# Matmul order inside a weight unit, and eight placements of the moving tiles

## The chip, the cores and the metric

The kernel runs on one core of a Trainium2 chip. The metric is the device time of one execution in microseconds (us). Times before are the median of three runs; the profile is of one more execution.

## The reference

One inference step of a decoder trunk of one layer, width 2048, for 256 prompt tokens and 8 x 4 sample tokens (288 token columns in all). Three sub-layers follow each other, each inside RMS norms: a SwiGLU feed-forward pair, a hybrid mixer (a gated linear attention group and an HGRN2 group, both recurrences), and a second SwiGLU pair.

```python
x = x + 0.5 * rmsnorm(swiglu(rmsnorm(x, g[0]), ffn1_w_in, ffn1_w_out), g[1])
m, sg, sh = hybrid_mixer(rmsnorm(x, g[2]), mix_w_in, ..., mix_w_out, s_gla, s_hgrn)
x = x + rmsnorm(m, g[3])
x = x + 0.5 * rmsnorm(swiglu(rmsnorm(x, g[4]), ffn2_w_in, ffn2_w_out), g[5])
# swiglu(x) = (silu(x @ w_gate) * (x @ w_up)) @ w_out, hidden width 5632
```

Everything is float32, and the weights are large: 364 MB are read from memory.

## The kernel before, in words

Activations lie transposed: a tile holds 128 features (partitions) by 288 tokens, so x is 16 tiles (`KT = 16`). To reach float32 accuracy with the faster float32r matmul, each operand is split into a high and a low part, and a product is three matmuls, recorded at L596, L597 and L598: weights high by x high, weights high by x low, weights low by x high. The parts of x are `xh[k]` and `xl[k]`; those of the hidden layer are `hh` and `hl`.

The class `Weights` streams the weights in units of 128 x 1024 numbers: SyncE loads a unit (`raw`, 3 buffers), ACT writes its high part (L100) and DVE its low part (L101) into a `wh` buffer (`hl` in the code, 4 buffers, at times 2 more on the other side of the memory). One buffer holds two halves `a` of `HALF = 1024 + 32` numbers, each with 512 high numbers, 512 low numbers and a gap of 32. A unit covers two tiles of x (`k` and `k + 1`, one half each) for four output tiles of 128 features.

The function `block` computes four output tiles (`f = 0..3`) over `nk` tiles of x: `nk / 2` units, the products of one output tile being summed in one bank. It walks the units in order. In all but the last unit it takes `k` outermost and `f` inside; in the last unit (`tail`) it takes `f` outermost and `k` inside, and evacuates each output tile (`evac`) as it is finished. After each `k` it calls `tick(k)`, in which other blocks' work is issued: squares for a norm, steps of the recurrence, splits. The feed-forward stages are made of `gate`, `up` (8 units each, on x) and `out` blocks (2 units each, on the hidden tiles); the mixer has blocks `qk`, `v`, `hfq`, `hi`, `gate` and `mo`, all on x or on the mixer's output, which takes the place of x in `xh` and `xl`. The first block of each stage (`gate1_0`, `qk0`, `gate2_0`) has orders of its own: `fill` puts products that are ready early first, `late` holds some back.

The order on each engine is the order of issue, with marks (`issue_after`) that place an instruction behind another; there is no loop at run time. In the mixer's last gate block `tick_last` writes the high and low parts of the mixer's output `y` over `xh` and `xl` (`split_y`), tile by tile, as soon as the block has read them.

In the program, each partition holds first `x`, `y`, then `xh[0..15]`, `xl[0..15]`, `rt`, `rp`, `acc`, `cols`, then the raw buffers and the weight buffers. A tile of x takes 288 x 4 = 1152 bytes. The extra weight buffers and the fill tiles lie at the other end, behind a tile named `gap`, and their places follow its size.

Of the kernel before, what the change touches and what calls it, by code (L numbers as in the profile page):

```python
# [9 lines left out]
F32 = mybir.dt.float32  # L10
F32R = mybir.dt.float32r
# [5 lines left out]
P = 128  # L17
TP = 256
TS = 32
T = TP + TS  # L20
# [3 lines left out]
KT = D // P  # L24
# [106 lines left out]
def trunk_kernel(ctx, tc, x_prompt, x_sample, state_gla, state_hgrn, norm_gains, f1_in, f1_out, f2_in, f2_out,  # L131
# [6 lines left out]
    xpool = ctx.enter_context(tc.tile_pool(name="xpool", bufs=1))  # L138
# [104 lines left out]
    FIRST = 2  # L243
# [4 lines left out]
    x = [xpool.tile([P, T], F32, name=f"x{k}") for k in range(KT)]  # L248
    yg = [xpool.tile([P, 4, T], F32, name=f"y{k}") for k in range(4)]
    y = [yg[k // 4][:, k % 4, :] for k in range(KT)]  # L250
    xh = [xpool.tile([P, T], F32R, name=f"xh{k}") for k in range(KT)]
    xl = [xpool.tile([P, T], F32R, name=f"xl{k}") for k in range(KT)]
    rt = xpool.tile([P, T], F32, name="rt")
    rp = xpool.tile([P, T], F32, name="rp")
    acc = xpool.tile([P, T], F32, name="acc")
    cols = xpool.tile([P, 16], F32, name="cols")

    def gain(i, k):
        return prm[:, i * KT + k:i * KT + k + 1]
# [324 lines left out]

    product = [None]

    def block(name, nk, rhs, evac, width=512, tick=None, tail=1, hold=False, most=99, fill=None, late=0):

        nf, per = width // P, 1024 // width
        nu = nk // per  # L590
        ps = [mmtile(f"{name}_{f}") for f in range(nf)]
        ws = [W.next() for _ in range(EARLY // per)] if fill else []

        def mm3(dst, w, f, k, parts, start, stop):
            a, c = k % per, slice(f * P, f * P + P)
            yield lambda: PE.matmul(dst, w[0][:, a, c], parts[0], start=start, stop=False)  # L596
            yield lambda: PE.matmul(dst, w[0][:, a, c], parts[1], start=False, stop=False)  # L597
            yield lambda: PE.matmul(dst, w[1][:, a, c], parts[0], start=False, stop=stop)  # L598

        def mm(w, f, k):  # L600
            if not fill or f or k >= EARLY:
                for ready in mm3(ps[f][:, 0:T], w, f, k, rhs(k), k == 0, k == nk - 1):
                    product[0] = ready().ins

        if fill:
            fill.products(lambda dst, k, parts, stop: mm3(dst, ws[k // per], 0, k, parts, k == 0, stop), ps[0][:, 0:T])
        for u in range(nu - tail):
            w = ws.pop(0) if ws else W.next()
            for k in range(u * per, (u + 1) * per):
                if fill and k < UPDATED:  # L610

                    fs = range(1 if k < EARLY else 0, nf)
                    threes = [list(mm3(ps[f][:, 0:T], w, f, k, rhs(k), k == 0, False)) for f in fs]
                    for three in threes:
                        three[0]()
                        product[0] = three[2]().ins
                    with tc.issue_after(product[0]):
                        for three in threes:
                            product[0] = three[1]().ins
                elif k < late:  # L620

                    threes = [list(mm3(ps[f][:, 0:T], w, f, k, rhs(k), k == 0, False)) for f in range(nf)]
                    for ready in [r for t in threes for r in t[:2]] + [t[2] for t in threes]:
                        product[0] = ready().ins
                else:
                    for f in range(nf):
                        mm(w, f, k)
                if tick is not None:
                    tick(k)
            W.ahead(most)  # L630
            if fill and u == 5:
                fill.scaled()
        ws = [W.next() for _ in range(tail)]
        ks = range((nu - tail) * per, nk)
        ticked = 0
        for f in range(nf):
            for k in ks:
                mm(ws[k // per - (nu - tail)], f, k)
            evac(f, fill.total(ps[f][:, 0:T]) if fill and f == 0 else ps[f][:, 0:T])
            while tick is not None and (ticked + 1) * nf <= (f + 1) * len(ks):  # L640
                tick(ks[ticked])
                ticked += 1
        if not hold:
            W.ahead()
# [4 lines left out]
    def ffn(tag, gcol, gnext, pn, before, fill=None):  # L649
# [3 lines left out]
        with ExitStack() as pools:  # L653
# [3 lines left out]
            def do_in(c):  # L657
                hh = fp.tile([P, 4, T], F32R, name=f"hh{tag}_{c}", tag="hh")
                hl = fp.tile([P, 4, T], F32R, name=f"hl{tag}_{c}", tag="hl")
                hid[c] = (hh, hl)  # L660
                gs = []

                def gate(g):
                    def run():
                        V.tensor_tensor(g, g, rt, op=ALU.mult)
                        act(g, g, AF.Silu)
                    return run

                def ev_gate(f, ps):
                    g = fp.tile([P, T], F32, name="g", tag="g", bufs=6)  # L670
                    gs.append(g)
                    if c == 0:
                        W.behind = S.activation(g, ps, AF.Copy).ins
                        pn.late.append(gate(g))
                    else:
                        V.tensor_tensor(g, ps, rt, op=ALU.mult)
                        act(g, g, AF.Silu)

                def ev_up(f, ps):
                    u = fp.tile([P, T], F32, name="u", tag="u", bufs=3)  # L680
                    V.tensor_tensor(u, ps, rt, op=ALU.mult)  # L681
                    V.tensor_tensor(u, u, gs[f], op=ALU.mult)
                    S.activation(hh[:, f, :], u, AF.Copy)
                    V.tensor_tensor(hl[:, f, :], u, hh[:, f, :].bitcast(F32), op=ALU.subtract)

                if c == 0:
                    block(f"gate{tag}_0", KT, xrhs, ev_gate, tick=pn.tick0, most=1 if final else 0, fill=fill,
                          late=0 if final else FIRST)
                    before.close()
                    if not final:  # L690
                        border.append(Border(mixer_start, hg1, gnext, 5, 2))
                else:
                    block(f"gate{tag}_{c}", KT, xrhs, ev_gate)
                if final and c == 0:
                    last_pool()
                block(f"up{tag}_{c}", KT, xrhs, ev_up, tick=pn.tick1 if c == 0 else None)
# [170 lines left out]
    def mixer(pn, border):  # L867
        with ExitStack() as mx:
# [667 lines left out]
            for g in range(2):  # L1536
                d = group_tiles(f"g{g}")
                block(f"qk{g}", KT, xrhs, ev_gla(d, g == 0), tick=tick if g else pn.tick0, most=99 if g else 1,
                      fill=None if g else border.fill)
                if g == 0:  # L1540
                    scan_pool()
                if g == 0:
                    vt = vtiles("g0")
                    block("v0", KT, xrhs, ev_v(*vt, 2, yg[1]), 
                          tick=lambda k: (pn.tick1(k), scale_lr() if k == 8 else a_lr() if k == 10 else lr_parts() if k == 12 else None))
                    with tc.issue_after(W.recent[0]), tc.issue_after(W.recent[1]):
                        lower_bounds()

                    turns.insert(0, lambda d=d: gla_decay(d, 0))
                else:  # L1550
                    turns.extend([lambda d=d, f=f: gla_decay(d, 1, (f,)) for f in range(2)])
                    vt = vtiles("g1")
                    block("v1", KT, xrhs, ev_v(*vt, 2, yg[1]), tick=tick)
                gens.append((g, scan(d, *vt, True, 4 * g, state_gla[0][:, 2 * g:2 * g + 2],
                                     sgp[0, 0, 2 * g:2 * g + 2], sgs[0][:, 2 * g:2 * g + 2]), True))
# [42 lines left out]
            def split_y(t):  # L1598
                S.activation(xh[t], y[t], AF.Copy)
                V.tensor_tensor(xl[t], y[t], xh[t].bitcast(F32), op=ALU.subtract)  # L1600
# [6 lines left out]
                    tick(k)  # L1607

            def tick_last(k):
                if k < 12:  # L1610
                    split_y(k)

            for n in range(4):
                block(f"gate{n}", KT, xrhs, ev_gate(n), tick=(tick, tick, tick_silu, tick_last)[n])
# [22 lines left out]
    class Border:  # L1637


        def __init__(self, n, gains, gnext, some, ahead=0):  # L1640
            self.pools = ExitStack()
            top = self.pools.enter_context(tc.tile_pool(name=f"top{gnext}", bufs=1, side="right"))
            top.tile([P, 56], F32, name=f"gap{gnext}")
            W.begin_extra(self.pools.enter_context(tc.tile_pool(name=f"hx{gnext}", bufs=2, side="right")), wider(n))
            self.fill = Fill(self.pools.enter_context(tc.tile_pool(name=f"fl{gnext}", bufs=1, side="right")),
                             f"fill{gnext}", gains, gnext, some, ahead)
# [47 lines left out]
```

## Time and profile before

| what | us |
|---|---|
| median of 3 runs | 2227.61 |
| lowest and highest run | 2226.94, 2229.22 |
| the profiled execution | 2226.28 |
| its span | 2224.5 |
| TensorE matmul busy | 2212.8 (17,820 matmuls) |
| TensorE weight load busy | 2197.9 (17,820) |
| VectorE (DVE) busy | 1386.7 |
| ScalarE (ACT) busy | 1020.1 |
| GpSimd (POOL) busy | 180.2 |

The span is the time from the first to the last instruction of the profiled execution; the execution's own time has 1.8 us around it. Busy times are those of instructions in flight. Matmuls are pipelined, so one matmul's duration (about 290 ns) covers parts of its neighbours; how fast they follow each other is read from the differences of their starts. A row of the timeline has the start, the duration, the engine, the line, the operation and its operands; a row of the groups has the count behind the x, then busy us and the mean ns of one, then the idle time before. A row of the waits says who waited for whom, for how many us in all, how often, and the longest.

### The profile page before, as it was taken

Reading aid. Unit: us, or ns where it says so; the run is one execution under the profiler, and the core shown is the slowest. Engines: PE = TensorE matmul, PEld = TensorE weight load, DVE = VectorE, ACT = ScalarE, POOL = GpSimd, SP = SyncE. Lnnn points to the kernel's source line nnn. Section 1 sums busy time; section 2 is a strip of 40 time slices with the busy share of each in tenths; the row PEclk is TensorE's granted clock in tenths of the full one; section 3 lists DMA queues with packets and bytes.
Section 4 is the critical chain, followed back from the end, with each engine's and each line's share of the span. In section 5 each row is a group of like instructions: output and inputs, shape, how many; then the busy total and the mean of one; then the engine's idle time right before and its main releaser. Section 6 shows DMA issues by size and latency. Waiting matters only on the chain. (4 is left out here: it accounts for less than half of the span.)

```text
span 2224.5 us, 43196 instructions
## 1 busy us (share of the span) xinstructions
PE 2212.8 (99%) x17820; PEld 2197.9 (99%) x17820; DVE 1386.7 (62%) x2254; ACT 1020.1 (46%) x1535; POOL 180.2 (8%) x327
## 2 busy tenths in 40 slices
PE   9999999999999999999999999999999999999998
PEld 9999999999999999999999999999999999999998
DVE  7645546554555568888888755844555466556646
ACT  6453333333334345655676654543333333333344
POOL 2000000000000001233210000000000020122005
PEclk9999999999999999999999999999999999999999
DMA  7555555555555554667566564555555565566555
GB/s 224 173 166 167 170 167 166 170 165 168 171 164 181 177 165 139 193 204 214 171 188 179 174 185 133 171 168 165 170 167 165 170 176 168 179 178 176 171 162 159
DMA packets 227334, 384.87 MB, mean 173 GB/s; under 512 B 21362, under 2 KB 60864, under 8 KB 227136
## 3 DMA queue, kind: packets, MB, share of 16 engines
q1 hardware_dynamic: 213776, 364.89, 54.8%
q0 software_dynamic: 10992, 16.77, 2.9%
q8 instruction: 140, 2.29, 0.4%
q10 hardware_dynamic: 2368, 0.44, 0.1%
q14 instruction: 58, 0.48, 0.1%
HBM read 363.75 MB, written 11.80 MB: 169 GB/s over the span
## 5 line engine op out<-in xcount | busy, mean ns | idle before, releaser
L101 DVE TENSOR_TENSOR wh<-raw,wh 128x1024 fp32r<-128x1024 f32 (+1 forms) x676 | 821.8, 1217 | 619.0 <-ACT wh L100 617.5
L100 ACT ACTIVATE wh<-raw 128x1024 fp32r<-128x1024 f32 (+1 forms) x676 | 711.0, 1053 | 961.0 <-PE gate L598 301.8
L596 PE MATMUL gate<-xh,wh 128*128 128x288 f32 x1660 | 485.5, 294 | 0.0
L598 PE MATMUL gate<-xh,wh 128*128 128x288 f32 x1660 | 484.8, 293 | 0.0
L597 PE MATMUL gate<-xl,wh 128*128 128x288 f32 x1660 | 484.7, 294 | 0.0
L597 PE MATMUL out<-hl,wh 128*128 128x288 f32 x1408 | 416.2, 296 | 0.0
L597 PE MATMUL up<-xl,wh 128*128 128x288 f32 x1408 | 413.9, 294 | 0.0
L598 PE MATMUL up<-xh,wh 128*128 128x288 f32 x1408 | 412.8, 293 | 0.0
L598 PE MATMUL out<-hh,wh 128*128 128x288 f32 x1408 | 412.1, 293 | 0.0
L596 PE MATMUL up<-xh,wh 128*128 128x288 f32 x1408 | 411.8, 293 | 0.0
L596 PE MATMUL out<-hh,wh 128*128 128x288 f32 x1408 | 411.5, 292 | 0.0
L596 PEld LDWEIGHTS gate<-xh,wh 128*128 128x128 f32 x1660 | 311.2, 188 | 0.8 <-DVE u L681 0.4
L598 PEld LDWEIGHTS gate<-xh,wh 128*128 128x128 f32 x1660 | 311.1, 188 | 0.2 <-DVE wh L101 0.2
L597 PEld LDWEIGHTS gate<-xl,wh 128*128 128x128 f32 x1660 | 310.5, 188 | 0.5
L596 PEld LDWEIGHTS out<-hh,wh 128*128 128x128 f32 x1408 | 264.9, 188 | 0.0
L596 PEld LDWEIGHTS up<-xh,wh 128*128 128x128 f32 x1408 | 264.4, 188 | 0.0
L597 PEld LDWEIGHTS out<-hl,wh 128*128 128x128 f32 x1408 | 264.3, 188 | 0.0
L598 PEld LDWEIGHTS out<-hh,wh 128*128 128x128 f32 x1408 | 264.3, 188 | 0.0
L597 PEld LDWEIGHTS up<-xl,wh 128*128 128x128 f32 x1408 | 264.2, 188 | 0.0
L598 PEld LDWEIGHTS up<-xh,wh 128*128 128x128 f32 x1408 | 264.2, 188 | 0.0
L770 DVE TENSOR_TENSOR y<-out,y 128x288 f32<-128x288 f32 x287 | 120.7, 452 | 85.2 <-PE out L598 84.1
L727 POOL DMA_DIRECT2D xT<-b x64 | 37.2, 588 | 764.8 <-PE gate L598 571.8
(410 smaller groups left out, 2550.3 us busy)
## 6 DMA issues: line engine op xcount, KB each, us to landing
raw<-in_ffn_w_in_dram SPq DMA_DIRECT2D x350, 512.0 KB, 3.6
raw<-in_ffn_w_out_dram SPq DMA_DIRECT2D x176, 512.0 KB, 3.6
raw<-in_mix_w_in_dram SPq DMA_DIRECT2D x64, 512.0 KB, 4.1
raw<-in_mix_w_in_dram SPq DMA_DIRECT2D x96, 256.0 KB, 3.2
raw<-in_mix_w_out_dram SPq DMA_DIRECT2D x32, 512.0 KB, 3.8
out_dram<-s POOLq DMA_DIRECT2D x32, 256.0 KB, 2.9
s<-in_state_gla_dram SPq DMA_DIRECT2D x16, 256.0 KB, 4.9
s<-in_state_hgrn_dram SPq DMA_DIRECT2D x16, 256.0 KB, 5.2
```

What stands on the lines that cost most here:

```text
L100: i1 = self.nc.scalar.activation(h[:, a, c], raw[:, a, c], AF.Copy).ins
L101: i2 = self.nc.vector.tensor_tensor(l[:, a, c], raw[:, a, c], h[:, a, c].bitcast(F32), op=ALU.subtract).ins
L596: yield lambda: PE.matmul(dst, w[0][:, a, c], parts[0], start=start, stop=False)
L597: yield lambda: PE.matmul(dst, w[0][:, a, c], parts[1], start=False, stop=False)
L598: yield lambda: PE.matmul(dst, w[1][:, a, c], parts[0], start=False, stop=stop)
L727: queues[n % len(queues)].dma_start(dst[q * TS:(q + 1) * TS, 4 * g:4 * g + 4, :, cols].rearrange("p k t c -> p (k t) c"), b32[rows, q])
L770: V.tensor_tensor(y[k], ps, y[k], op=ALU.add)
```

## The change

Inside every unit but the last, `block` now takes the output tile `f` outermost and the unit's two tiles of x inside, as the last unit did before, and calls `tick` after the second and the fourth output tile. The first block of each stage keeps the old order (`byk=True`). `xh` and `xl` become two single tiles in which the tiles of x lie at growing steps: those of unit u are moved up by `step[u]` numbers of 4 bytes. The weight buffers move up by 544 bytes, since these two tiles have 64 spare numbers each and `cols` grows by 8; `gap` shrinks by 8. So the distance from the weights to the tiles of x, modulo 256 bytes, which was 64 for all units, becomes 32, 48, 56, 64, 72, 80, 96 and 112 for units 0 to 7. The hidden tiles keep 64. `tick_last` splits each tile two calls later.

```diff
-    xh = [xpool.tile([P, T], F32R, name=f"xh{k}") for k in range(KT)]
-    xl = [xpool.tile([P, T], F32R, name=f"xl{k}") for k in range(KT)]
+    step = (0, 4, 6, 8, 10, 12, 16, 20)
+    xall = [xpool.tile([P, KT * T + 64], F32R, name=f"x{p}") for p in "hl"]
+    xh, xl = [[t[:, k * T + step[k // 2]:k * T + step[k // 2] + T] for k in range(KT)] for t in xall]
...
-    cols = xpool.tile([P, 16], F32, name="cols")
+    cols = xpool.tile([P, 24], F32, name="cols")
...
-    def block(name, nk, rhs, evac, width=512, tick=None, tail=1, hold=False, most=99, fill=None, late=0):
+    def block(name, nk, rhs, evac, width=512, tick=None, tail=1, hold=False, most=99, fill=None, late=0, byk=False):
...
         for u in range(nu - tail):
             w = ws.pop(0) if ws else W.next()
-            for k in range(u * per, (u + 1) * per):
+            if not byk:
+                for f in range(nf):
+                    for k in range(u * per, (u + 1) * per):
+                        mm(w, f, k)
+                    if tick is not None and f % 2:
+                        tick(u * per + f // 2)
+            for k in range(u * per, (u + 1) * per) if byk else ():
...
             def tick_last(k):
-                if k < 12:
-                    split_y(k)
+                if 2 <= k < 14:
+                    split_y(k - 2)
...
-            top.tile([P, 56], F32, name=f"gap{gnext}")
+            top.tile([P, 48], F32, name=f"gap{gnext}")
```

The calls of `block` for `gate{tag}_0` and for `qk0` pass `byk=True`.

More of the change, by code (lines that the diff above doesn't have):

```diff
@@ L687, in do_in @@
                     block(f"gate{tag}_0", KT, xrhs, ev_gate, tick=pn.tick0, most=1 if final else 0, fill=fill,
-                          late=0 if final else FIRST)
+                          late=0 if final else FIRST, byk=True)
                     before.close()
@@ L1538, in mixer @@
                 block(f"qk{g}", KT, xrhs, ev_gla(d, g == 0), tick=tick if g else pn.tick0, most=99 if g else 1,
-                      fill=None if g else border.fill)
+                      fill=None if g else border.fill, byk=not g)
                 if g == 0:
```

## The prediction

> **What bounds the kernel now.** I read the page's engine shares first, then the clock row, then the waits of the engines, and last the order of time of TensorE inside single blocks, because everything else points there.
>
> ```profile
> PE 2212.8 (99%) x17820; PEld 2197.9 (99%) x17820; DVE 1386.7 (62%) x2254; ACT 1020.1 (46%) x1535; POOL 180.2 (8%) x327
> PEclk9999999999999999999999999999999999999999
> ACT wh L100 <- PE gate L598: 301.8, 150, 2.3
> PE warm L311 <- POOL onesD L233: 1.1, 1, 1.1
> ```
>
> TensorE is busy for 99% of the span at the full clock in all 40 slices. ACT, which splits the weights, waits for TensorE (301.8 us in front of one kind of block alone), while the longest wait of TensorE itself is 1.1 us, once, at the start. So weights come early, and the time is the number of matmuls times the interval from one start to the next. The chain that ended last says nothing more: it is the output's last 0.1%.
>
> The counts come from the groups of instructions, the forms kept apart. L596, L597 and L598 are the three products (high by high, high by low, low by high), each with the same count as its L596 row.
>
> ```profile
> L596 PE MATMUL gate<-xh,wh 128*128 128x288 f32 x1660 | 485.5, 294 | 0.0
> L596 PE MATMUL up<-xh,wh 128*128 128x288 f32 x1408 | 411.8, 293 | 0.0
> L596 PE MATMUL out<-hh,wh 128*128 128x288 f32 x1408 | 411.5, 292 | 0.0
> L596 PE MATMUL hfq<-xh,wh 128*128 128x288 f32 x256 | 76.9, 301 | 0.0
> L596 PE MATMUL mo<-xh,wh 128*128 128x288 f32 x256 | 74.9, 293 | 0.0
> L596 PE MATMUL hi<-xh,wh 128*128 128x288 f32 x128 | 38.3, 299 | 0.0
> L596 PE MATMUL v<-xh,wh 128*128 128x288 f32 x128 | 38.2, 298 | 0.0
> L596 PE MATMUL qk<-xh,wh 128*128 128x288 f32 x124 | 34.7, 298 | 0.6 <-DVE y L1000 0.4
> ```
>
> Tiles of x stream in 3 x (1660 + 1408 + 256 + 256 + 128 + 128 + 124) = 11,880 matmuls; the hidden tiles hh and hl in 3 x 1408 = 4,224. The durations in these rows overlap, so they are not the price. The price is the difference of starts, from the timeline of one up block (192 matmuls) and the start of the out block behind it:
>
> ```profile
> 161.87 0.29 PE L596 MATMUL up<-xh,wh 128*128 128x288 f32 x1
> 166.60 0.29 PE L596 MATMUL up<-xh,wh 128*128 128x288 f32 x1
> ...
> 183.95 0.29 PE L596 MATMUL up<-xh,wh 128*128 128x288 f32 x1
> ...
> 185.14 0.29 PE L596 MATMUL up<-xh,wh 128*128 128x288 f32 x1
> 185.26 0.30 PE L597 MATMUL up<-xl,wh 128*128 128x288 f32 x1
> 185.40 0.29 PE L598 MATMUL up<-xh,wh 128*128 128x288 f32 x1
> 185.53 0.29 PE L596 MATMUL up<-xh,wh 128*128 128x288 f32 x1
> ...
> 187.09 0.29 PE L596 MATMUL out<-hh,wh 128*128 128x288 f32 x1
> 190.24 0.29 PE L596 MATMUL out<-hh,wh 128*128 128x288 f32 x1
> 193.38 0.29 PE L596 MATMUL out<-hh,wh 128*128 128x288 f32 x1
> ```
>
> The rows are the starts of matmuls 0, 36, 168, 177, 178, 179, 180 and 192 of the block. The whole block took 187.09 - 161.87 = 25.22 us, 131.35 ns a matmul. The stretch in the old order (each tile of x against four output tiles), 36 to 168, took 17.35 us for 132: 131.4 ns. The last unit (168 to 192) is already worked by output tile: 3.14 us for 24, 130.8 ns. Inside it the first nine took 1.19 us, 132.2 ns, and the last fifteen 1.95 us, 130.0 ns, in a pattern of about 0.12, 0.14, 0.13 us that repeats with the three products. So the kernel itself shows the new order, at one placement, and it shows that the pattern takes about nine matmuls to settle.
>
> **Why order and placement can matter.** While a matmul streams its 288 columns of x, the next weights (128 columns) are read from the same memory. In the program of the kernel before, xh0 starts at byte 55,616 of each partition and the first weight buffer at 108,288: modulo 256 that is 64 and 0. A tile of x takes 1,152 bytes and a weight half-slot 4,224, both 128 modulo 256, and xl lies 18,432 (72 x 256) behind xh; so x lies 64 bytes behind its weights everywhere, the hidden tiles too. In the old order nearly every matmul streams x while weights at distance 64 are loaded. By output tile, the third product of each tile streams x while the other tile's weights are loaded, at 64 + 128. That is the only difference of the two orders to the memory, and the interval goes from 131.4 to 130.0 ns.
>
> [...]
>
> **The change, part by part.** The bigger x storage (two tiles with 256 bytes of slack each, cols 32 bytes longer) moves the weight buffers by 544 bytes, 32 modulo 256; the gap tile on the other side shrinks by 32, so that the extra weight buffers and the fill tiles follow. The steps 0, 4, 6, 8, 10, 12, 16, 20 floats then put the eight units at 32, 48, 56, 64, 72, 80, 96 and 112. The hidden tiles move along with the weights and stay at 64.
>
> *Out blocks* (4,224 matmuls): order alone changes. Now 193.38 - 187.09 = 6.29 us for 48, 131.0 ns. After: 130.0, with nine unsettled matmuls (2.2 ns more each) in every 192 behind the up block, 130.1. 4,224 x -0.95 ns = -4.0 us. This is the surest term.
>
> *Blocks on x.* Three blocks (the first gates, the first qk) keep the old order: 3 x 192 = 576; 11,880 - 576 = 11,304 change order, and all change placement. No row shows a steady stretch at another placement. The nearest rows for a unit of 24: it settles as now, 130.8; or it does not, and stays at the unsettled 132.2. That the same three products need not settle shows in the fill products, which come in this order at 64 (and 64 + 128), first, last and next:
>
> ```profile
> 846.21 0.29 PE L596 MATMUL fill<-fill2yh,wh 128*128 128x288 f32 x1
> 847.67 0.30 PE L598 MATMUL fill<-fill2yh,wh 128*128 128x288 f32 x1
> ...
> 1378.86 0.29 PE L596 MATMUL fill<-fill4yh,wh 128*128 128x288 f32 x1
> 1380.44 0.29 PE L596 MATMUL gate<-xh,wh 128*128 128x288 f32 x1
> ```
>
> Eleven intervals in 1.46 us are 132.7 ns, twelve in 1.58 us are 131.7, together 132.2. Each unit starts with a new placement, so the nine unsettled matmuls come eight times a block. I take half the units as settling: (130.8 + 132.2) / 2 = 131.5, against 131.35 now: 11,304 x +0.15 = +1.7 us. The ends, all or none: -6.2 and +9.6 us. The three blocks in the old order lose the one placement under which they ran: at 132.2, 576 x 0.85 = +0.5 us.
>
> *Ticks and splits.* Two ticks a unit remain, each after twelve matmuls, so the side work keeps its times: 0. In the last gate block the splits of y (an ACT copy and a DVE subtraction, no DMA) come one unit later, since the old tile is read until the unit ends.
>
> ```profile
> ACT xh L1599 <- PE gate L598: 7.6, 11, 1.1
> ```
>
> They wait for TensorE now (7.6 us in 11 waits); later they wait less. Splits 10 and 11 then land in the seventh unit instead of the sixth; the next block starts on tiles 0 and 1, and tiles 12 to 15 are split behind the block as before. Cover: the six units (144 products, 19 us at 131 ns) that the next block works before it reads tile 12. Without it, two waits of the longest kind in that row, 1.1 us each. Merging the x tiles costs nothing if waits follow regions, as they do for y, stored four to a tile. Taken at 0.
>
> *Sum*: -4.0 + 1.7 + 0.5 = -1.8 us on the profiled execution's 2226.28 (span 2224.5), 2224.5. The median of the runs is 2227.61, 1.33 above it: 2225.8, say 2226.
>
> **The rivals.** *Order counts, placement hardly* (chance 0.26): the short pattern carries on from unit to unit. All at 130.0: 11,304 x -1.35 = -15.3, the out blocks 4,224 x -1.04 = -4.4, the three old-order blocks +0.5, together -19.2 us: 2208; settling anew in each unit (130.8) gives -9.7: 2218. For it: the pattern returns at every block's end. Against: the fill products do not reach it, and the trace has it at one placement only. [...]
>
> *Slower: placements away from 64 collide more* (chance 0.35). Its place is seven of eight units. The nearest rows are matmuls of the scan and the norm at other distances: pairs of 256 columns, the first at 96 bytes from the weights loaded beside it, the second at 64, and a pair of 288 columns at 128.
>
> ```profile
> 963.33 0.41 PE L1347 MATMUL sn<-Vsg,bd 96*128 96x256 f32 x2
> 963.58 0.29 PE L596 MATMUL v<-xh,wh 128*128 128x288 f32 x1
> ...
> 1024.97 0.40 PE L1347 MATMUL sn<-Vsg,bd 96*128 96x256 f32 x2
> 1025.21 0.30 PE L596 MATMUL hi<-xh,wh 128*128 128x288 f32 x1
> ...
> 1423.32 0.30 PE L465 MATMUL pre<-nh,onesR 128*128 128x288 f32 x1
> 1423.59 0.29 PE L596 MATMUL up<-xh,wh 128*128 128x288 f32 x1
> ```
>
> The pairs of 256 columns took 0.25 and 0.24 us, 122.5 ns for one; scaled by 288/256 that is at most 137.8. The pair of 288 took 0.27 us, 135 for one at this resolution. They are isolated, so part of this is lack of settling: between them and the 131.4 of now I take 133.5. Seven units at 133.5 and one at 130.8 are 133.2: 11,304 x 1.85 = +20.9, less 4.0, plus 1.2 for the three old-order blocks at 133.5: +18 us, 2246. It decides from a mean of 131.7 on x (break-even); 132.1 is slower by 0.2%.
>
> *The change does not do what it says* (0.02): region waits are lost in the merged tile and TensorE waits for splits; x is split anew four times, 64 tiles, and if a third of them cost the 1.1 us of the row above, 2250.
>
> **How the numbers follow.** The forecast has 0.37, and its own range is that between all and no units settling: 2218 to 2234. I count 0.2% (4.5 us) as what a measurement of this kernel can tell. That is below 2223.1 and above 2232.1: of the 16 us of the forecast's range 5 lie faster, 9 within and 2 slower, of its 0.37 so 0.12, 0.20 and 0.05. Faster 0.26 + 0.12 = 0.38; same 0.20; slower 0.35 + 0.02 + 0.05 = 0.42. The range takes in most of both rivals: 2210 to 2246, leaving out about a tenth on each side.
>
> **What would show it.** In the timeline of an out block of after, 24 matmuls should take 3.12 us in both halves (3.15 and 3.14 now). In an up block the eight units should differ: 3.14 us where the pattern of three settles, 3.17 where not; the fourth unit, still at 64, should be 3.14. Equal units at 3.12 speak for the first rival, units over 3.20 for the second, and idle time of TensorE in front of a product with DVE as releaser for the third. I am wrong if the out blocks do not gain, or if units at one distance differ from block to block.

## The result and the profile after

The changed kernel takes 2238.93 us (median of 3 runs, 2238.83 to 2239.31) against 2227.61 before: 11.3 us slower, ratio 1.0051 with a 95% interval of 1.0037 to 1.0065. The profiled execution took 2239.31 us, its span 2237.4. What bounds it did not move; these are the page's engine row and clock row of after, and the longest waits of TensorE.

```profile
PE 2224.8 (99%) x17820; PEld 2210.9 (99%) x17820; DVE 1386.8 (62%) x2254; ACT 1022.6 (46%) x1535; POOL 180.3 (8%) x327
PEclk9999999999999999999999999999999999999999
PE warm L312 <- POOL onesD L233: 1.1, 1, 1.1
PE postf L832 <- DVE sq L773: 0.6, 2, 0.4
```

The same 17,820 matmuls are in flight for 12.0 us more, at the same mean granted clock (0.998 before and after), and no wait of TensorE of more than 0.3 us is new. So the loss lies again in the interval from one matmul's start to the next. The timeline of one up block of after, the first product of each of its eight units, and of the out block behind it:

```profile
163.72 0.29 PE L597 MATMUL up<-xh,wh 128*128 128x288 f32 x1
166.91 0.29 PE L597 MATMUL up<-xh,wh 128*128 128x288 f32 x1
170.09 0.30 PE L597 MATMUL up<-xh,wh 128*128 128x288 f32 x1
173.32 0.30 PE L597 MATMUL up<-xh,wh 128*128 128x288 f32 x1
176.46 0.29 PE L597 MATMUL up<-xh,wh 128*128 128x288 f32 x1
179.69 0.29 PE L597 MATMUL up<-xh,wh 128*128 128x288 f32 x1
182.85 0.30 PE L597 MATMUL up<-xh,wh 128*128 128x288 f32 x1
186.01 0.30 PE L597 MATMUL up<-xh,wh 128*128 128x288 f32 x1
189.23 0.29 PE L597 MATMUL out<-hh,wh 128*128 128x288 f32 x1
192.38 0.29 PE L597 MATMUL out<-hh,wh 128*128 128x288 f32 x1
195.50 0.29 PE L597 MATMUL out<-hh,wh 128*128 128x288 f32 x1
```

The block takes 25.51 us instead of 25.22. Its units (24 matmuls each) take 3.19, 3.18, 3.23, 3.14, 3.23, 3.16, 3.16 and 3.22 us: each placement has a price, and the fourth unit, still at 64 bytes, has the lowest. The out block's second unit takes 3.12 us. Summed over all blocks from the differences of starts, the 4,224 products of the out blocks went from 554.0 to 549.8 us (-4.2), and those that stream x, with the few fill products, grew by 16.2 us: together +12.0.

For the tables below I took the same differences for each unit number in the 20 up blocks that no other work interrupts, and their means: for the whole unit, and for its last twelve matmuls, where the pattern has settled in most units. The settled values of the experiments are read in the same way.

| unit of after | 0 | 1 | 2 | 3 | 4 | 5 | 6 | 7 | mean |
|---|---|---|---|---|---|---|---|---|---|
| distance, bytes | 32 | 48 | 56 | 64 | 72 | 80 | 96 | 112 | |
| whole unit, ns | 132.7 | 132.4 | 134.7 | 130.9 | 134.4 | 132.1 | 131.4 | 134.2 | 132.85 |
| last twelve, ns | 132.2 | 132.2 | 135.6 | 130.0 | 134.4 | 132.2 | 131.1 | 134.4 | |

Against the 131.35 of before, 56, 72 and 112 bring 3.4 + 3.0 + 2.9 = 9.3 of the 12.0 ns that the eight units lose together.

### The profile page after: what moved, and what is told of

The parts are those of the page before. It is cut to its first block, busy times and chain, and to the rows that moved or that the text cites. A ratio compares the mean times of both kernels' runs of the same rounds, so it can differ in the third digit from the quotient of the medians.

```text
span 2237.4 us, 43194 instructions
## 1 busy us (share of the span) xinstructions
PE 2224.8 (99%) x17820; PEld 2210.9 (99%) x17820; DVE 1386.8 (62%) x2254; ACT 1022.6 (46%) x1535; POOL 180.3 (8%) x327
```

## The experiments

Edits are shown against the changed kernel. Theory A throughout: the interval follows from the distances between the x that streams and the weights that load beside it, product after product.

**1. Order alone.** All units back at 64.

```diff
-    step = (0, 4, 6, 8, 10, 12, 16, 20)
+    step = (8,) * 8
```

> The new order with all eight units put back to 64 bytes (step 8 for all; the two merged x tiles, the longer cols and the shorter gap stay). Theory A, placement: each unit has its own steady pattern, set by the distance between the tile of x that streams and the weights that load; at 64 it is 130.0 ns, so x blocks fall from 131.35 to about 130.0 and the out blocks to 130.1: 2208 us, ratio to before 0.991. Rival B, order or merging costs: the new order itself (or the merged tiles) makes x blocks slow, then this stays near the changed kernel, 2235 to 2240, ratio 1.004.

2211.39 us against 2228.78 for the kernel before, measured beside it, ratio 0.9923 (0.9906 to 0.9939). The order, the merged tiles, the moved buffers and the later splits together gain 17 us; the placements turn this into 11 us of loss. In this run's timeline, the first two rows are the start and the end of an up block, the last two those of a mo block:

```profile
161.61 0.29 PE L597 MATMUL up<-xh,wh 128*128 128x288 f32 x1
186.57 0.29 PE L597 MATMUL out<-hh,wh 128*128 128x288 f32 x1
...
1292.64 0.29 PE L597 MATMUL mo<-xh,wh 128*128 128x288 f32 x1
1318.03 0.29 PE L597 MATMUL mo<-xh,wh 128*128 128x288 f32 x1
```

The up block takes 24.96 us for 192, 130.0 ns throughout. The mo block, of the same order and the same distances, takes 25.39 us, 132.2. That was not expected. The four mo blocks, 768 matmuls at 2.2 ns, make 1.7 us of this profiled execution, which took 2213.29 us, so they explain at most half of the 3 us by which the median lies above the 2208 of theory A; the rest was not followed up. Experiment 7 takes up the mo blocks.

**2. Placement alone.** The old order in all blocks (the last unit of each keeps its own), with the eight distances.

```diff
-def block(..., late=0, byk=False):
+def block(..., late=0, byk=True):
```

> The eight distances alone, with the old order (tile of x outermost) in all blocks but the last unit of each. Theory A: slower than before, since out blocks gain nothing and seven units leave 64: units differ in the timeline, mean of x blocks 132 to 135, time 2235 to 2265. Rival B (order is what costs): as before, 2227 to 2229, units all at 131.4.

2243.19 us, ratio 1.0066 (1.0051 to 1.0081): placement alone costs 14 us in the old order. The block's start, its fourth unit's first product, the fifth's, and the block's end:

```profile
163.76 0.29 PE L597 MATMUL up<-xh,wh 128*128 128x288 f32 x1
...
173.34 0.30 PE L597 MATMUL up<-xh,wh 128*128 128x288 f32 x1
176.49 0.29 PE L597 MATMUL up<-xh,wh 128*128 128x288 f32 x1
...
189.24 0.29 PE L597 MATMUL out<-hh,wh 128*128 128x288 f32 x1
```

25.48 us for the block, 3.15 for the unit at 64, as before. The four kernels in one table (medians; the changed kernel was measured at another time, beside 2227.6 for the kernel before):

| | all at 64 | eight distances |
|---|---|---|
| old order | 2228.8 | 2243.2 |
| by output tile | 2211.4 | 2238.9 |

**3. Far placements, and low parts placed apart from high parts.** Two runs at other distances.

```diff
-    step = (0, 4, 6, 8, 10, 12, 16, 20)
+    step = (24, 32, 36, 40, 44, 48, 52, 56)
```

> The new order with the eight units at 128, 160, 176, 192, 208, 224, 240 and 256 (0 modulo 256) bytes, to read a steady interval for each. Theory A: each unit settles to a pattern of its own between 130 and 136 ns, the same in every block, with no relation to its number in the block; since the third product then meets 0 to 128, a unit at 192 need not equal the one at 64. Rival B: all units near the 132.85 mean of the changed kernel's up blocks.

```diff
+    steps = (8,) * 8, (0, 16, 24, 32, 40, 48, 56, 60)      # of xh, of xl
```

> The new order with xh at 64 in all units, and xl alone at 32, 96, 128, 160, 192, 224, 256 and 272 (16 modulo 256). Theory A: units differ although xh stays, since the second product (high by low) streams xl while the low weights load; between 129 and 136 ns. A unit that beats 130.0 shows that the high and low parts want different places. Rival C, only the first and third product matter: all units at 130.0.

2240.63 us for the first, one run. Settled: 132.2 (128), 132.8 (160), 132.2 (176), 133.3 (192), 132.6 (208), 133.3 (224), 129.9 (240), 132.8 (0). Units differ and 240 is a second good place, so rival B (all near 132.85) falls there; the other seven lie within 0.7 ns of it. 192, the partner of 64, is not good. 2236.06 us for the second. Settled: 134.7, 133.3, 132.2, 132.2, 133.0, 132.2, 132.6, 131.1: none beats 130.0, and rival C (only the first and third product matter) falls, since xh was at 64 in all of them. The gate blocks of the first run, many of them interrupted by other work, agree with its up blocks within 0.9 ns except at 160 (130.6 against 132.8), so theory A's "the same in every block" did not hold to the letter there. Its up block around unit 6, and an out block:

```profile
181.79 0.29 PE L597 MATMUL up<-xh,wh 128*128 128x288 f32 x1
184.93 0.29 PE L597 MATMUL up<-xh,wh 128*128 128x288 f32 x1
...
194.46 0.29 PE L597 MATMUL out<-hh,wh 128*128 128x288 f32 x1
200.81 0.29 PE L597 MATMUL out<-hh,wh 128*128 128x288 f32 x1
```

Unit 6 takes 3.14 us, its way into the pattern included. The out block takes 6.35 us for 48, 132.2 ns, although hidden tiles and weights lie as in experiment 1, where out blocks ran at 130.0. So placement and order do not fix the interval alone.

**4. One unit out of eight misplaced.** Does the unit in front of the out blocks decide?

```diff
-    step = (0, 4, 6, 8, 10, 12, 16, 20)
+    step = (8,) * 7 + (56,)
```

> The new order, seven units at 64 and the eighth alone at 256 (0 modulo 256), the hidden tiles at 64. In the run with far placements the out blocks took 132.2 ns although nothing of theirs was changed (same order, still 64), entered from a unit at 0. Theory D, two patterns: at 64 the stream has a short pattern (130.0) and a long one (132.2), each holds once entered, and which one depends on what ran before. Then out blocks, and the first units of the gate or up block behind a unit at 0, stay at 132.2 for whole units. Rival E, placement alone decides: all units at 64 and all out blocks return to 130.0 within about ten matmuls, only the eighth unit is at 133.

2213.58 us, one run. Theory D's forecast fell: everything behind the unit at 0 returned to 130.0, in the out blocks and in the units at 64, after about fifteen matmuls. The eighth unit's start, the out block's start, and a later out block's start and end:

```profile
183.38 0.29 PE L597 MATMUL up<-xh,wh 128*128 128x288 f32 x1
186.56 0.29 PE L597 MATMUL out<-hh,wh 128*128 128x288 f32 x1
...
192.83 0.29 PE L597 MATMUL out<-hh,wh 128*128 128x288 f32 x1
199.07 0.29 PE L597 MATMUL out<-hh,wh 128*128 128x288 f32 x1
```

3.18 us for the misplaced unit, 6.24 (130.0 ns) for the out block. A unit at 0 in front is thus not enough to hold out blocks at 132.2; what held those of experiment 3 stays open.

**5. Distance, or x's own place on the 16-byte grid?** In the changed kernel 56 and 72, the two slowest as whole units, are also the two whose x starts 8 bytes off a multiple of 16 (112, on that grid, settles as slowly as 72). The grid, multiples of 16 bytes, is here a guess that these two units suggest. Here the weights move by 8 bytes.

```diff
-        h, l = hl[:, :, 0:512], hl[:, :, 512:1024]
+        h, l = hl[:, :, 2:514], hl[:, :, 514:1026]
```

> The changed kernel with the weights inside their buffers moved up by 8 bytes, so every distance falls by 8: units at 24, 40, 48, 56, 64, 72, 88 and 104, and the out blocks at 56. Units 2 and 4 (x off the 16-byte grid before and now) get 48 and 64. Theory F, distance: unit 4 takes 130.0 to 130.9 and unit 2 132.2 (as 64 and 48 did), unit 3 134.7 and unit 5 134.4 (as 56 and 72), out blocks 134 to 136. Rival G, x off the 16-byte grid is what was slow at 56 and 72: units 2 and 4 stay at 134 to 135 and unit 3, on the grid, is faster than 134.

```diff
-    step = (0, 4, 6, 8, 10, 12, 16, 20)
+    step = (1, 3, 5, 7, 9, 11, 13, 22)
```

> The changed kernel with finer distances: 36, 44, 52, 60, 68, 76, 84 and 120. Theory F, distance by 16-byte steps: all of these lie between multiples of 16 and take 132 to 136, 60 and 68 as well, so that 64 is a narrow dip. Rival: a smooth dependence, with 60 and 68 near 130 to 131.

2243.82 and 2250.08 us, one run each. Starts of units 2 to 7 of an up block of the first, and its end:

```profile
169.70 0.30 PE L597 MATMUL up<-xh,wh 128*128 128x288 f32 x1
172.89 0.29 PE L597 MATMUL up<-xh,wh 128*128 128x288 f32 x1
176.05 0.30 PE L597 MATMUL up<-xh,wh 128*128 128x288 f32 x1
179.29 0.30 PE L597 MATMUL up<-xh,wh 128*128 128x288 f32 x1
182.47 0.30 PE L597 MATMUL up<-xh,wh 128*128 128x288 f32 x1
185.66 0.30 PE L597 MATMUL up<-xh,wh 128*128 128x288 f32 x1
188.78 0.29 PE L597 MATMUL out<-hh,wh 128*128 128x288 f32 x1
```

Unit 3, at 56 with x on the grid, takes 3.16 us; unit 4, at 64 with x and weights both 8 bytes off it, 3.24 (135.0 ns). So 64 is not good when x and weights are both off the grid, and theory F (distance alone) falls. Rival G gets units 3 and 4 right, but not unit 2, off the grid at 48: 3.19 us, settled at 132.2. Unit 7, at 104, takes 3.12 us and settles at 130.0, a third good place, with x on the grid and the weights off it; in the change the same x, at 112, settled at 134.4. In the second run all x lie off the grid; settled, its units took 135.9 (36), 131.1 (44), 134.4 (52), 132.2 (60), 135.6 (68), 130.6 (76), 135.6 (84) and 135.6 (120). Neither forecast for it held: 44 and 76 came out below 132, and 60 and 68 are not near 130. The out blocks of the first, now at 56 with x on the grid, took 132.2. Together, over the up blocks of this and the other runs in the new order with xh and xl placed alike (the change, experiments 3, 5 and 8, each combination counted once), 12 settled units with x off the grid average 134.1 ns and 22 on it 132.2. Off the grid is worse on average, but each combination has its own value: 76 bytes, off the grid, settled at 130.6. Why the averages differ was not measured.

**6. The order of distances.** Within an output tile the products of the two tiles alternate, so all of them meet distance + 128.

```diff
+                    threes = [list(mm3(ps[f][:, 0:T], w, f, k, rhs(k), k == 0, False)) for k in range(u * per, (u + 1) * per)]
+                    for ready in [t[p] for p in range(3) for t in threes]:
+                        product[0] = ready().ins
```

> The changed kernel's eight placements, but inside an output tile the products of the unit's two tiles alternate (high by high of both, high by low of both, low by high of both). Every product then streams x while weights at distance + 128 load, the same for all: 160, 176, 184, 192, 200, 208, 224, 240. Theory A: the order as such has no price, the sequence of distances has; units with one distance throughout settle to patterns between 126 and 136 ns, the out blocks (192 throughout) to one of their own, not 130.0. Rival B, products by output tile are worth 130.0 whatever the distances: out blocks stay at 130.1.

2260.41 us, one run, the slowest of all: units settled at 133.3, 132.2, 135.1, 132.2, 136.7, 136.7, 134.4 and (the last, which keeps the change's order) 134.4. The sixth unit's first product and the seventh's; then the starts of the two units of an out block:

```profile
180.69 0.30 PE L597 MATMUL up<-xh,wh 128*128 128x288 f32 x1
183.96 0.29 PE L597 MATMUL up<-xh,wh 128*128 128x288 f32 x1
...
196.73 0.29 PE L597 MATMUL out<-hh,wh 128*128 128x288 f32 x1
199.91 0.29 PE L597 MATMUL out<-hh,wh 128*128 128x288 f32 x1
```

3.27 us, against 3.16 for the same placement (80) in the change's order. The two units at 136.7 lie above the 136 that theory A allowed. The first unit of the out blocks took 3.18 us, 132.5 ns, no longer 130: working by output tile is not enough by itself, and rival B falls. That the sequence of distances makes the difference fits, but is not shown by this run, which changes the order of high and low products along with it.

**7. Two patterns at one placement, and the second good distance.** All at 64 with the first mo block in the old order; and all at 240.

```diff
-    step = (0, 4, 6, 8, 10, 12, 16, 20)
+    step = (8,) * 8
...
-            block(f"mo{o}", KT, xrhs, ev, tail=2 if o == 3 else 1, hold=o == 3)
+            block(f"mo{o}", KT, xrhs, ev, tail=2 if o == 3 else 1, hold=o == 3, byk=not o)
```

> All units at 64 and the new order, as in the first experiment, where the mo blocks ran at 132.2 ns although order and placement were those of the up blocks at 130.0. Here the first mo block has the old order in its first seven units; its last unit then enters the new order as every block of the kernel before did. Theory D, at one order and placement there are two lasting patterns and the entry picks one: mo1 to mo3 fall to 130.0, 576 x 2.2 = 1.3 us, 2210 us, ratio 0.9917. Rival: something in the mo blocks themselves makes 132.2 (their evacuation, the weights' buffers), then mo1 to mo3 stay and the time is 2211 to 2212.

```diff
-    step = (0, 4, 6, 8, 10, 12, 16, 20)
+    step = (52,) * 8
```

> The new order with all units at 240, the distance beside 64 at which a unit settled at 130 ns (in the run with far placements). Theory A: gate and up blocks at 130.0 to 130.6, the time within 3 us of the 2211.4 of all units at 64. Rival: what a unit takes depends on the units around it, then the blocks are at 131 to 133 and the time is 2220 to 2235.

2210.83 us for the first, ratio 0.9923 (0.9906 to 0.9939), not to be told apart from experiment 1 by time; by the trace it can. Its second mo block:

```profile
1291.09 0.29 PE L597 MATMUL mo<-xh,wh 128*128 128x288 f32 x1
1316.05 0.29 PE L597 MATMUL mo<-xh,wh 128*128 128x288 f32 x1
```

24.96 us, 130.0 ns, where experiment 1 had 25.39: nothing in this block was changed, only what ran in front of it. So at one order and placement two patterns last, 130.0 and 132.2, and the rival (something in the mo blocks themselves) falls. That the entry picks the pattern is not shown. The programs of experiments 1 and 7 are the same up to the first mo block, yet a v block 400 us ahead of it already differs; two of its products, 108 matmuls apart, in experiment 1:

```profile
868.39 0.29 PE L597 MATMUL v<-xh,wh 128*128 128x288 f32 x1
882.67 0.29 PE L597 MATMUL v<-xh,wh 128*128 128x288 f32 x1
```

and the same two here:

```profile
867.47 0.29 PE L597 MATMUL v<-xh,wh 128*128 128x288 f32 x1
881.51 0.29 PE L597 MATMUL v<-xh,wh 128*128 128x288 f32 x1
```

14.28 us are 132.2 ns, 14.04 are 130.0. An up block behind the mo blocks, also unchanged, came out the other way round: 130.0 in experiment 1, 132.2 here. So which pattern a stretch keeps can change from one execution to the next without an edit, and with one profiled execution of each kernel, whether the edit or chance brought the mo blocks to 130.0 stays open.

2210.68 us for the second, ratio 0.9922 (0.9907 to 0.9937): 240 is as good as 64. The rival, that a unit's value hangs on its neighbours, falls for this distance. Both beat the kernel before and the changed one; between the three versions at 2211 the times do not decide.

**8. The same distances at other unit numbers.**

```diff
-    step = (0, 4, 6, 8, 10, 12, 16, 20)
+    step = (8, 8, 12, 20, 28, 28, 52, 60)
```

> The new order with units at 64, 64, 80, 112, 144, 144, 240 and 272 (16 modulo 256): 80 and 112 now in units 2 and 3 instead of 5 and 7. Theory A, placement: once settled they take again 132.2 and 134.4; both units at 144 alike; 64 at 130.0. Rival, the unit's number in the block (its weights' arrival, the ticks) decides: units 2 and 3 near the 135.5 and 130.0 that stood there in the changed kernel.

2226.70 us, one run. Starts of units 2 to 7 (80, 112, 144, 144, 240, 16):

```profile
168.41 0.30 PE L597 MATMUL up<-xh,wh 128*128 128x288 f32 x1
171.59 0.29 PE L597 MATMUL up<-xh,wh 128*128 128x288 f32 x1
174.79 0.29 PE L597 MATMUL up<-xh,wh 128*128 128x288 f32 x1
177.97 0.30 PE L597 MATMUL up<-xh,wh 128*128 128x288 f32 x1
181.14 0.29 PE L597 MATMUL up<-xh,wh 128*128 128x288 f32 x1
184.26 0.30 PE L597 MATMUL up<-xh,wh 128*128 128x288 f32 x1
```

Settled, 80 takes 132.2 and 112 takes 134.4 again, now in units 2 and 3; both units at 144 take 132.2; 240 takes 3.12 us for the unit, 130.0. The rival (the unit's number) falls.

## Why the prediction was wrong

- **What bounds the kernel, the price per interval**: right. 12.0 of the 12.9 us by which the span grew are 17,820 matmuls at another spacing; no wait over 0.3 us came.
- **Out blocks, -4.0 us**: measured -4.2. Halves of 3.12 us were forecast; they are 3.15 and 3.12, the first with the way into the pattern behind a unit at 112.
- **Blocks on x, +1.7 us**: this is the step that failed. With the three blocks in the old order, for which +0.5 was forecast and the differences of starts give about +0.6, they took +16.2, so this term measured about +15.6. I let a unit lie between 130.8 (settles) and 132.2 (does not), both of which came from rows at 64. But a unit at another distance does not fail to settle: it settles, mostly within ten to fifteen matmuls, into a slower pattern. Five of eight units lie above my upper end, 56, 72 and 112 by 2.0 to 2.5 ns. The mean was 132.85, not 131.5; 11,304 times the difference turns -1.8 into +13.4, against 11.3 between the medians and 13.0 between the profiled executions.
- **The rival that placements away from 64 are slower**: right in that these placements cost more, and by the sign named for it: three units lie over 3.20 us (3.23, 3.23 and 3.22). That anything collides there is the author's reading; the runs show the intervals alone. It took 133.5 for seven units and 133.2 in the mean, 2246 us, from isolated pairs; measured 132.85 and 2239. That it came so near is partly luck. One of the two pairs of 256 columns lay at 64 itself; the other, at 96, gave 125 ns, 140.6 when scaled to 288 columns, and the pair of 288 at 128 gave 135, while units at 96 and 128 settled at 131.1 and 132.2. What these rows could say is that no upper end may be drawn from rows at 64; the fill products, from which it was drawn, lie at 64 and could not say anything on placement.
- **The first rival** (order counts, placement hardly), 2208 if all units took 130.0: refuted as a reading of the change, but experiment 1 gives its number when the placements are taken out: 2211.
- **No cost for ticks, splits and the merged tiles**: none was seen. They are all in experiment 1, which is faster, and the longest wait of TensorE matmuls on a split of x there is 0.2 us.

That placement costs is shown by experiments 1 and 2: 2238.9 against 2211.4 us in the new order, 2243.2 against 2228.8 in the old, with nothing else of weight changed. That it is not x's own address alone is shown by experiment 5: its x lie where the change has them and only the weights moved, by 8 bytes, and unit 7 went from 134.4 to 130.0 and unit 4 from 134.4 to 135.6. That the distance alone is not enough is shown there too, by the unit at 64. Between 130.0 and 132.2 some care is due, since 64 was seen at both (experiment 7): that 32, 48 and 80 are worse places than 64 rests on their coming out alike in all 20 up blocks of an execution, and 80 also in experiment 8. What makes the interval longer at one place than at another was not measured, and why 64, 240 and 104 are good stays open. A kernel in which the third product meets the same distance as the other two was not tried.

## What to carry to other kernels

When TensorE is busy for the whole span, read the difference of starts to a nanosecond and compare it between stretches of equal work: about 1.1 ns on 16,000 matmuls was 17 us here (experiment 1). The place of the moving tile against the weights that load beside it is a parameter to be scanned (here it moved the settled interval from 130.0 ns at 64 to 135.6 at 56), eight placements in one run read off unit by unit, and the best one then used for all; a scan is no version to keep. For a forecast, do not bound the price of a new placement by rows at the old one, however well measured; a few isolated rows at other placements show at most that the price can lie outside.

## What the runs showed of the hardware

- Settled units lie mostly on steps: 130.0, 131.1, 132.2, 133.3, 134.4, 135.6 ns, that is in the mean 390.0 ns for three products plus a multiple of 3.3. Some lie between, such as 132.6 (208), 132.8 (160 and 0) and 130.6 (76).
- A stream of equal matmuls can keep one of two spacings at the same order and placement, 130.0 or 132.2 ns, for a block of 192 matmuls (mo blocks: 25.39 us in experiment 1, 24.96 in experiment 7), and two executions of the same stretch of program can differ in it (108 matmuls of the v block: 14.28 us in experiment 1, 14.04 in experiment 7).
- At a mean granted clock of 0.998 (both profiles), the same products of the up blocks cost between 130.0 and 134.4 ns in the mean by placement and order alone (experiments 1 and 6), 3%.
- Weights load beside the stream: in the trace of before, the load for the next product (PEld) starts with the matmul in front of it.

```profile
900.09 0.29 PE L596 MATMUL qk<-xh,wh 128*128 128x288 f32 x1
900.09 0.19 PEld L597 LDWEIGHTS qk<-xl,wh 128*128 128x128 f32 x1
```

- Distances that differ by multiples of 256 bytes came out alike: in before, the first seven units of the 20 up blocks, with tiles of x 2304 (9 x 256) bytes apart from unit to unit and weight buffers 8448 (33 x 256) apart, all took 131.4 ns a matmul.
- A float32 matmul took longer than a float32r one: in the trace of before, the last three of `warm` (float32, 128 columns) start at 5.69 us and the product behind them at 6.28, 0.20 us for one, where a float32r matmul of 288 columns takes 0.13.
